# Tensor sums of a one-core mixer layer from GpSimd to VectorE, six pairs of them made early, and a new order of projections

## The chip, the core and the metric

The kernel runs on one core of one Trainium2 chip. The metric is the time of one execution on the device in microseconds; three runs of the kernel before gave 1037.36, 1037.79 and 1039.32, median 1037.79.

A core has a matrix engine (TensorE, PE in the profile; its weight loads are PEld), a vector engine (VectorE, DVE), an engine for pointwise functions (ScalarE, ACT) and a programmable one (GpSimd, POOL). Each works through its own list of instructions in the order in which the program has them, and waits on semaphores for the others. A fifth queue (SyncE, SP) issues nearly all DMAs.

## The reference

One layer over 512 tokens of width 2048, all in float32. The names in brackets are the one-letter names of the kernel's units.

```python
proj = x @ w_in                                     # (512, 2048) @ (2048, 8320)
rw, hg = proj[:, :4224], proj[:, 4224:]
rw = rw + shift_mu * (previous_token(rw) - rw)
r, k, v, z, wd, ad = split(rw)                      # [r k v z], 1024 each; [w] = wd and ad, 64 each
decay = exp(-exp(-softplus(-(w0 + tanh(wd) @ w_decay_up)) - 0.5))
a = sigmoid(a0 + ad @ a_up)
# RWKV-7, 16 heads of 64: per token S <- S * decay - (S kk)(kk a)^T + v k^T, o = S r
o_rwkv = (group_norm(o) + bonus(r, k, v)) * silu(z)
q, f, i, zh = split(hg)                             # [q f i g], 1024 each
# HGRN2, 8 heads of 128, chunks of 64 tokens: gated linear recurrence with gates from f
o_hgrn = rms_norm(hgrn2(silu(q), f, i)) * g_norm_w * silu(zh)
y = concat(o_rwkv, o_hgrn) @ w_out                  # (512, 2048) @ (2048, 2048)
out = layer_norm(2 ** 0.25 * x + y) * ln_w + ln_b
```

## The kernel before

*Products.* Every large product is made three times in a reduced float format: both factors are split into a high part (ACT copies) and a low part (DVE subtracts, line 377 through `split`), and PE adds high x high, high x low and low x high (`three`, line 524). A 128x512 tile of weights is read from DRAM into `wr`, split into `wh` and `wl`, and two parts are split ahead of the one in use. `xh` and `xl` hold the split tokens, and later the split gated channels.

*Units.* The input projection is 59 units. All but two are one tile of 128 channels over all tokens (48 large products), named by a letter and a number: `w0` (the low-rank inputs), `k`, `r`, `v`, `z` for the eight pairs of RWKV heads, `q`, `f`, `g` for the eight HGRN heads; `i0` and `i1` are four tiles each. `_order()` says in which order they are made. Their results start the other work: `rwkv_prep` (from `k`, `r`), `rwkv_group` (two pairs at a time: inversion of a triangular matrix, then the scan over eight chunks), `rwkv_finish` (needs `z`), `hgrn_heads` (from `q`, `f`), `hgrn_out` (needs `i`, `g`). Each head or pair ends as a gated tile in a buffer `g`, of which there are four; the first twelve to be used are written to DRAM (`put_gated`, tile `spill`) and read back when the output projection comes (`reload`).

*The order of the instructions* is fixed when the program is built. A class `Plan` keeps a clock for each engine, with constants for the cost of an operation, and the work is written as generators in queues. Between any two large products the planner goes through the queues and issues the instructions whose operands are ready by its clocks. The weight splits come first among the queues, the weight sums (below) last. `fetched` sets when a load is expected: 0.44 us for the issue, size over 360 GB/s, and 1.8 us more. A small product that would interrupt the large ones alone is held for up to `HOLD`, so that others can join it. For the last six units (`HURRY`) nothing is held.

*The output projection* is made in four column blocks of 512. Block 0 and block 3 are plain products. Blocks 1 and 2 are made with seven products instead of eight over blocks of tokens and of weight tiles (`PASSES`), and these need sums and differences of tiles on both sides:

- Weight sums (`weight_sums`): 16 loads of four tiles, four subtractions of 128x256 each on GpSimd (line 409 through `pool_tt`), and a store to DRAM (`sums_w`). Two generators share the work, each with one of the two `inv` buffers; the inversions use the same two buffers later.
- Token sums (`union`): for each of eight pairs of channel tiles, two tiles are read again from `spill` (the last two pairs are still in SBUF), and four sums of 128x256 are made on GpSimd. `alone` then splits them into high and low parts.
- The scaled residual 2^0.25 x is added to a partial result by `join`, eight times: ACT scales the tile `x_r` in place, GpSimd adds it.

`row_out` does the residual of the other tiles in one DVE instruction. The layer norm runs behind each row block; the last row's tail is `finish_last`.

Of the kernel before, what the change touches and what calls it, by code (L numbers as in the profile page):

```python
# [7 lines left out]
F32 = mybir.dt.float32  # L8
F32R = mybir.dt.float32r
U8 = mybir.dt.uint8  # L10
AF = mybir.ActivationFunctionType
ALU = mybir.AluOpType
# [3 lines left out]
P = 128  # L16
T = 512
# [3 lines left out]
NPAIR = 8  # L21
# [6 lines left out]
ALPHA = 2.0 ** 0.25  # L28
# [8 lines left out]

def _order():  # L40

    o = [("w", 0)]
    for g in range(NPAIR // 2):
        for p in (2 * g, 2 * g + 1):
            o += [("k", p), ("r", p)]
            if g:
                o.append(("z", p - 2))
            o.append(("v", p))
        o += [("q", 2 * g), ("f", 2 * g), ("q", 2 * g + 1), ("f", 2 * g + 1)]
        if g % 2 == 0:  # L50
            o.append(("i", g // 2))
        o += [("g", 2 * g), ("g", 2 * g + 1)]
    return o + [("z", NPAIR - 2), ("z", NPAIR - 1)]


PASSES = (("B11", "A11"), ("B21", "A12"), (3, "S2"), (0, "S1"), ("B22", "S4"), (1, "S3"), (2, "A22"))
# [8 lines left out]
class Plan:  # L65
# [4 lines left out]

    AFTER = {"pe": 0.2, "act": 0.145, "dve": 0.13, "pool": 0.06, "dma": 0.0, None: 0.1}
    TO_PE = 0.12
    HOLD = {"whole": 0.6, "narrow": 0.6}
    TURN = 0.215
    REST = 1.5
    LEAD = -0.35
# [186 lines left out]
def mixer_kernel(ctx, tc, head, x_r, w_all, par, up, ln_wb, consts, hmask, out):  # L263
# [19 lines left out]
    plan = Plan({**BUFS, **PBUFS})  # L283
# [5 lines left out]
    def take(tag, shape=(P, T), dt=F32):  # L289

        if not plan.free(tag):
            raise RuntimeError(f"no room: {tag}")
        slot = min(plan.slots[tag])
        plan.slots[tag].remove(slot)
        if tag in PBUFS:
            t = ppool.tile(list(shape), dt, tag=tag, name=nm(tag), bufs=PBUFS[tag])
            plan.banks.add(t.tensor.name)
        else:
            t = st(tag, list(shape), dt)
        name = t.tensor.name  # L300
        plan.busy[name] = (slot[1], None)
        tags[name] = tag
        return t

    def drop(*tiles):
        for t in tiles:
            name = t.tensor.name
            plan.slots[tags.pop(name)].append((plan.used.get(name, plan.count), plan.busy[name][0]))

    def room(**need):  # L310

        return lambda: all(plan.free(tag, n) for tag, n in need.items())
# [17 lines left out]
    def send(o, i, cost=0.44):  # L330

        nc.sync.dma_start(o, i)
        plan.clock["sp"] = max(plan.clock["sp"], plan.clock["pe"]) + cost
# [36 lines left out]
    def act(o, i, f, scale=1.0, bias=0.0):  # L370
        return Op([act_way(o, i, f, scale, bias)], [i], [o], SETS.get(f))
# [4 lines left out]
    def tt(o, a, b, f=ALU.mult, base=None):  # L376
        return dve_op([a, b], o, lambda: dve.tensor_tensor(o, a, b, f),  # L377
                      base=base or 0.16 if o.shape[0] < P and size(o) == C and o.tensor.name in tags else 0.07)
# [10 lines left out]
    def stt(o, a, s, b, f1, f2):  # L389
        return dve_op([a, b], o, lambda: dve.scalar_tensor_tensor(o, a, s, b, f1, f2), per=0.00113,  # L390
                      base=0.085 if o.shape[0] == P and size(o) > P else 0.12 if o.shape[0] == P
                      else 0.21 if size(o) == C else 0.165)
# [18 lines left out]
    def pool_tt(o, a, b, f):  # L411
        return Op([pool_tt_way(o, a, b, f)], [a, b], [o])
# [116 lines left out]
    def by_now(t):  # L529

        n = t.tensor.name
        return n in plan.ready and plan.seen(n, "pe") <= plan.clock["pe"] + plan.LEAD
# [141 lines left out]
    SPILL = (0, 1, 2, 3, 4, 5, 8, 9, 10, 11, 12, 13)  # L674
    spill = dpool.tile([len(SPILL), P, T], F32, tag="spill", name="spill")

    def put_gated(k, g):

        gated[k] = g
        if k in SPILL:  # L680
            def run():
                yield lambda: by_now(g)
                send(spill[SPILL.index(k)], g)
                drop(g)

            plan.add(stores, run())
# [601 lines left out]
    def weight_sums(first):  # L1288
        yield room(inv=1)
        w = take("inv", [P, 4, QT // 2])  # L1290
        for i in range(first, NSUM, 2):
            m, h = divmod(i, 2)
            yield lambda: plan.clock["sp"] <= plan.clock["pe"] + 0.2
            send(w, w_all[nsent + i].rearrange("p (a c) -> p a c", a=4))
            plan.fetched(w, 4 * HALF)
            for o, a, b in ((0, 1, 0), (1, 3, 1), (3, 3, 0), (2, 2, 3)):
                yield pool_tt(w[:, o], w[:, a], w[:, b], ALU.subtract)
            yield lambda: by_now(w)
            yield lambda: plan.clock["sp"] <= plan.clock["pe"] + 0.2
            send(sums_w[:, :, m, h * QT // 2 : (h + 1) * QT // 2].rearrange("a p c -> p a c"), w)  # L1300
            there = plan.busy[w.tensor.name] = (plan.clock["sp"] + 4.5, "dma")
            yield lambda: there[0] <= plan.clock["pe"]
        drop(w)
# [137 lines left out]
    unions, alones = [plan.queue(), plan.queue()], [plan.queue(), plan.queue()]  # L1441
    union_raw, unioned, homes = {}, {}, {}
    lnw = []
    lo_t, hi_t = slice(0, T // 2), slice(T // 2, T)

    def union(m, r1, r2):
        if m < 4:
            if m == 0:
                yield room(big=1)
                homes["raw"] = take("big", [P, 8, T])  # L1450
            d1, d2 = (homes["raw"][:, 2 * m + i] for i in range(2))
        elif m < 6:
            yield room(zz=1)
            z = homes["raw", m] = take("zz", [P, 2, T])
            d1, d2 = z[:, 0], z[:, 1]
        else:
            yield room(t=2)
            d1, d2 = homes["raw", m] = take("t"), take("t")
        if m < 6:
            yield room(t=6)  # L1460
            r1, r2 = take("t"), take("t")
            for i, r in enumerate((r1, r2)):
                yield lambda: plan.clock["sp"] <= plan.clock["pe"] + 0.2
                send(r, spill[SPILL.index(korder[2 * m + i])])
                plan.fetched(r, 4 * T)
        yield pool_tt(d2[:, hi_t], r1[:, hi_t], r2[:, hi_t], ALU.add)
        yield pool_tt(d1[:, hi_t], r1[:, lo_t], r1[:, hi_t], ALU.subtract)
        yield pool_tt(d1[:, lo_t], d2[:, hi_t], r1[:, lo_t], ALU.subtract)
        yield pool_tt(d2[:, lo_t], r2[:, lo_t], d1[:, lo_t], ALU.subtract)
        drop(r1, r2)  # L1470
        union_raw[m] = {"S1": d2[:, hi_t], "S3": d1[:, hi_t], "S2": d1[:, lo_t], "S4": d2[:, lo_t]}

    def union_home(n, m):
# [111 lines left out]
    def keyed(op, reads, writes):  # L1585

        op.reads, op.writes = reads, writes
        return op
# [188 lines left out]
    def join(o, a=None):  # L1777

        y, k = ys[o[0]][o[1]], y_keys(o[0], o[1] * T, o[1] * T + T)
        a = a or o  # L1780
        ya, ka = ys[a[0]][a[1]], y_keys(a[0], a[1] * T, a[1] * T + T)
        yield lambda: o in xrs
        xr = xrs[o]
        yield act(xr, xr, AF.Copy, scale=ALPHA)
        yield keyed(pool_tt(y, ya, xr, ALU.add), ka + [xr.tensor.name], k)
        drop(xr)
        done.add(("joined", o))
        if o in ((0, 1), (1, 1)):
            plan.add(sums, rest(*o))
# [274 lines left out]
```

## Time and profile before

| | |
|---|---|
| median of 3 runs | 1037.79 us |
| the profiled execution: its time, its span | 1039.38 us, 1037.4 us |
| instructions in the profile | 18856 |
| PE, DVE, ACT, POOL busy | 1012.2, 859.5, 499.8, 151.3 us |
| DMA | 156.99 MB, 48.9% of the engines' time in the main queue |

The profile is of one execution, with the start and the duration of each instruction. Rows of groups read: source line, engine, operation, tiles written and read (buffer numbers left out), shape, count; then busy time in us and the mean of one in ns; then how long the engine stood idle just before them and what ended it. Large products overlap by about 0.17 us, since the profile models their ends, so their starts are what tells of PE's pace.

### The profile page before, as it was taken

The numbers are of one execution on the slowest core, as the hardware profiler recorded it, in microseconds if no ns is written. First come the engines' busy times: TensorE is split into PE (matmuls) and PEld (weight loads), VectorE is DVE, ScalarE is ACT, GpSimd is POOL, SyncE is SP. The second block draws the span as 40 slices with busy tenths as digits, with TensorE's granted clock in tenths as the row PEclk, the third lists the DMA queues.
The fourth block names the chain that finished last, engine by engine and source line by source line (L and its number), as shares of the span: only waits on it lengthen the run. The fifth ranks groups of instructions, "written<-read, shape, count | busy, mean of one in ns | idle before, by whom it ended". The sixth has DMA issues, their size and how long they took to land.

```text
span 1037.4 us, 18856 instructions
## 1 busy us (share of the span) xinstructions
PE 1012.2 (98%) x7076; PEld 830.2 (80%) x7076; DVE 859.5 (83%) x1815; ACT 499.8 (48%) x945; POOL 151.3 (15%) x182
## 2 busy tenths in 40 slices
PE   9999899999999999999999999999999999999996
PEld 7877788888888878888888888888888788777785
DVE  6687779877989988888999867867998998778857
ACT  6546342546363455555544353636245554355432
POOL 2454610000200010020001000100001003732001
PEclk9999999999999999999999999999999999999999
DMA  9668862232375432255463334363442345876734
GB/s 345 225 206 250 275 203 87 83 111 69 104 213 152 120 90 68 82 143 160 130 172 104 102 93 120 100 183 102 136 115 86 112 138 158 280 227 207 225 126 152
DMA packets 75434, 156.99 MB, mean 151 GB/s; under 512 B 10960, under 2 KB 34768, under 8 KB 75344
## 3 DMA queue, kind: packets, MB, share of 16 engines
q1 hardware_dynamic: 74912, 154.89, 48.9%
q8 instruction: 55, 0.90, 0.4%
q10 hardware_dynamic: 432, 0.92, 0.2%
q14 instruction: 35, 0.29, 0.1%
HBM read 128.91 MB, written 26.87 MB: 150 GB/s over the span
## 4 chain that ended last, share of the span: by engine, by line
PE 80%; DVE 10%; DMA 4%; issue 3%; ACT 1%; POOL 1%; SPq 0%; DVEq 0%; ACTq 0%; POOLq 0%
PE main L524 64%; PE mix L353 9%; PE main L1359 3%; DVE wl L377 2%; DVE q L377 2%; PE mix L524 2%; PE main L353 2%; DMA t<-spill 1%; DMA wr<-sums_w 1%; DVE t L377 1%; DMA g<-x_r 1%; DMA q<-far 1%; DMA q<-head 1%; DVE g L390 1%; DVE ksq L377 0%
## 5 line engine op out<-in xcount | busy, mean ns | idle before, releaser
L524 PE MATMUL main<-xh,wh 128*128 128x512 f32 x864 | 340.4, 394 | 0.0
L524 PE MATMUL main<-xh,wl 128*128 128x512 f32 x864 | 339.3, 393 | 0.1
L524 PE MATMUL main<-xl,wh 128*128 128x512 f32 x864 | 339.0, 392 | 0.0
L367 ACT ACTIVATE wh<-wr 128x512 fp32r<-128x512 f32 x293 | 182.6, 626 | 177.5 <-PE main L524 131.5
L377 DVE TENSOR_TENSOR wl<-wr,wh 128x512 fp32r<-128x512 f32 x293 | 205.4, 703 | 41.6 <-ACT wh L367 39.7
L524 PEld LDWEIGHTS main<-xh,wl 128*128 128x128 f32 x864 | 162.3, 188 | 34.2 <-DVE wl L377 0.6
L524 PEld LDWEIGHTS main<-xl,wh 128*128 128x128 f32 x864 | 162.4, 188 | 33.3 <-issue 0.6
L524 PEld LDWEIGHTS main<-xh,wh 128*128 128x128 f32 x864 | 162.3, 188 | 33.1
L524 PE MATMUL main<-wl,xh 128*128 128x512 f32 x200 | 78.9, 395 | 2.7 <-DVE wl L377 2.7
L524 PE MATMUL main<-wh,xh 128*128 128x512 f32 x200 | 78.9, 395 | 0.0
L524 PE MATMUL main<-wh,xl 128*128 128x512 f32 x200 | 78.5, 392 | 0.3 <-DVE xl L377 0.3
L409 POOL TENSOR_TENSOR inv<-inv 128x256 f32<-128x256 f32 x64 | 59.8, 937 | 73.3 <-DMA inv<-w_all 69.8
L416 POOL TENSOR_TENSOR sm<-sm,mhalf 128x8 f32<-128x8 f32 x8 | 18.5, 2318 | 200.8 <-DVE sm L386 150.7
L524 PEld LDWEIGHTS main<-wl,xh 128*128 128x128 f32 x200 | 37.7, 188 | 11.4 <-DVE wl L377 3.8
L524 PEld LDWEIGHTS main<-wh,xl 128*128 128x128 f32 x200 | 37.7, 189 | 8.3 <-DVE xl L377 0.7
L524 PEld LDWEIGHTS main<-wh,xh 128*128 128x128 f32 x200 | 37.7, 188 | 7.9
L377 DVE TENSOR_TENSOR inv<-inv,inv 64x30 f32<-64x30 f32 (+14 forms) x120 | 38.5, 321 | 2.9
L377 DVE TENSOR_TENSOR inv<-inv 64x30 f32<-64x30 f32 (+14 forms) x120 | 38.5, 321 | 2.4
L390 DVE SCALAR_TENSOR_TENSOR bd<-mix,pc,bd 64x64 f32<-64x64 f32 x112 | 31.7, 283 | 10.5 <-PE mix L353 8.3
L368 ACT ACTIVATE t<-main,om 128x512 f32<-128x512 f32 x33 | 22.1, 684 | 34.6 <-PE main L524 27.2
L377 DVE TENSOR_TENSOR t<-t,tot 128x256 f32<-128x256 f32 x96 | 37.9, 417 | 0.2
L367 ACT ACTIVATE t<-mix 64x128 f32<-64x128 f32 (+3 forms) x61 | 15.8, 262 | 43.6 <-DVE zz L377 23.7
(297 smaller groups left out, 1656.0 us busy)
## 6 DMA issues: line engine op xcount, KB each, us to landing
wr<-w_all SPq DMA_DIRECT2D x146, 512.0 KB, 3.8
inv<-w_all SPq DMA_DIRECT2D x16, 512.0 KB, 4.7
sums_w<-inv SPq DMA_DIRECT2D x16, 512.0 KB, 4.4
q<-head SPq DMA_DIRECT2D x14, 448.0 KB, 5.7
t<-spill SPq DMA_DIRECT2D x23, 256.0 KB, 4.3
far<-ksq SPq DMA_DIRECT2D x22, 256.0 KB, 3.3
wr<-sums_w SPq DMA_DIRECT2D x10, 512.0 KB, 5.4
far<-q SPq DMA_DIRECT2D x8, 512.0 KB, 4.3
```

Source lines behind the costliest of these rows:

```text
L353: return Op([("pe", cost, lambda: pe.matmul(o, l, r, start=start, stop=stop, **kw))], [l, r], [o], mode=("narrow", l.shape[0], 32 if m <= ...
L367: return "act", cost, lambda: sc_e.activation(o, i, f, scale=scale)
L368: return "act", cost, lambda: sc_e.activation(o, i, f, scale=scale, bias=bias)
L377: return dve_op([a, b], o, lambda: dve.tensor_tensor(o, a, b, f), base=base or 0.16 if o.shape[0] < P and size(o) == C and o.tensor.name i ...
L390: return dve_op([a, b], o, lambda: dve.scalar_tensor_tensor(o, a, s, b, f1, f2), per=0.00113, base=0.085 if o.shape[0] == P and size(o) > ...
L409: return "pool", 0.1 + size(o) * 0.0029, lambda: pool.tensor_tensor(o, a, b, f)
L416: lambda: pool.tensor_tensor(o, i, mhalf[:, : size(o)], ALU.pow))], [i], [o])
L524: pe.matmul(ps, l, r, start=first and i == 0, stop=last and i == 2)
L1359: pe.matmul(pss[a], *ops, start=k == 0 and low == of == 0, stop=k == KT - 1 and low == 1)
```

## The change

The order of the units is a list written out, `ORDER`, in place of the loop. Before it was `w0 k0 r0 v0 k1 r1 v1 q0 f0 q1 f1 i0 g0 g1 k2 r2 z0 v2 k3 r3 z1 v3 q2 f2 q3 f3 g2 g3 k4 r4 z2 v4 k5 r5 z3 v5 q4 f4 q5 f5 i1 g4 g5 k6 r6 z4 v6 k7 r7 z5 v7 q6 f6 q7 f7 g6 g7 z6 z7`. The holds go from 0.6 to 0.3 us (products that use the whole array) and 0.4 us (narrow ones). The four subtractions of a weight sum, and the four sums of a token pair, are issued on DVE. For the six pairs whose tiles go to DRAM, the sums are made when the second tile of the pair is gated, if three scratch tiles are free by then: the first tile is read back, the sums are written in place over both, and both go to DRAM (`sums_a`). `union` then reads these in place of the tiles. `join` is one DVE instruction.

```diff
+ORDER = (
+    "w0 k0 r0 q1 k1 r1 q0 v1 f1 v0 f0 g0 i0 g1 z0 k2 f2 r2 k3 r3 "
+    "v3 z1 v2 f3 q2 q3 z2 q5 g2 g3 r4 k4 k5 v4 v5 z3 f4 r5 q4 f5 "
+    "i1 g5 g4 k6 r6 v6 v7 z4 k7 r7 f6 q7 q6 f7 g6 z6 z5 g7 z7")
+
 def _order():
...
+    return [(u[0], int(u[1:])) for u in ORDER.split()]
...
-    HOLD = {"whole": 0.6, "narrow": 0.6}
+    HOLD = {"whole": 0.3, "narrow": 0.4}
...
+    spilled, early = {}, set()
+    sums_a = dpool.tile([len(SPILL) // 2, 2, P, T], F32, tag="sums_a", name="sums_a")
+    lo_t, hi_t = slice(0, T // 2), slice(T // 2, T)
+
+    def token_sums(r1, r2, d1, d2):
+
+        yield tt(d2[:, hi_t], r1[:, hi_t], r2[:, hi_t], ALU.add)
+        yield tt(d1[:, hi_t], r1[:, lo_t], r1[:, hi_t], ALU.subtract)
+        yield tt(d1[:, lo_t], d2[:, hi_t], r1[:, lo_t], ALU.subtract)
+        yield tt(d2[:, lo_t], r2[:, lo_t], d1[:, lo_t], ALU.subtract)
...
                 send(spill[SPILL.index(k)], g)
+                now = spilled[k] = plan.clock["sp"]
+                n = korder.index(k)
+                m, other = n // 2, korder[n ^ 1]
+                if other in spilled:
+                    yield lambda: plan.free("t", 3) or plan.clock["pe"] > now + 3.0
+                    if plan.free("t", 3):
+                        r = take("t")
+                        send(r, spill[SPILL.index(other)])
+                        plan.fetched(r, 4 * T)
+                        yield lambda: plan.clock["pe"] > now + 4.5
+                        r1, r2 = (r, g) if n % 2 else (g, r)
+                        yield from token_sums(r1, r2, r1, r2)
+                        for i, r_ in enumerate((r1, r2)):
+                            yield lambda: by_now(r_) and plan.clock["sp"] <= plan.clock["pe"] + 0.2
+                            send(sums_a[m, i], r_)
+                        early.add(m)
+                        drop(r)
                 drop(g)
...
             for o, a, b in ((0, 1, 0), (1, 3, 1), (3, 3, 0), (2, 2, 3)):
-                yield pool_tt(w[:, o], w[:, a], w[:, b], ALU.subtract)
+                yield tt(w[:, o], w[:, a], w[:, b], ALU.subtract)
...
-        if m < 6:
-            yield room(t=6)
-            r1, r2 = take("t"), take("t")
-            for i, r in enumerate((r1, r2)):
+        if m in early:
+            for i, d in enumerate((d1, d2)):
                 yield lambda: plan.clock["sp"] <= plan.clock["pe"] + 0.2
-                send(r, spill[SPILL.index(korder[2 * m + i])])
-                plan.fetched(r, 4 * T)
-        yield pool_tt(d2[:, hi_t], r1[:, hi_t], r2[:, hi_t], ALU.add)
-        yield pool_tt(d1[:, hi_t], r1[:, lo_t], r1[:, hi_t], ALU.subtract)
-        yield pool_tt(d1[:, lo_t], d2[:, hi_t], r1[:, lo_t], ALU.subtract)
-        yield pool_tt(d2[:, lo_t], r2[:, lo_t], d1[:, lo_t], ALU.subtract)
-        drop(r1, r2)
+                send(d, sums_a[m, i])
+                plan.fetched(d, 4 * T)
+        else:
+            if m < 6:
+                yield room(t=6)
+                r1, r2 = take("t"), take("t")
+                for i, r in enumerate((r1, r2)):
+                    yield lambda: plan.clock["sp"] <= plan.clock["pe"] + 0.2
+                    send(r, spill[SPILL.index(korder[2 * m + i])])
+                    plan.fetched(r, 4 * T)
+            yield from token_sums(r1, r2, d1, d2)
+            drop(r1, r2)
...
-        yield act(xr, xr, AF.Copy, scale=ALPHA)
-        yield keyed(pool_tt(y, ya, xr, ALU.add), ka + [xr.tensor.name], k)
+        yield keyed(stt(y, xr, ALPHA, ya, ALU.mult, ALU.add), ka + [xr.tensor.name], k)
         drop(xr)
```

More of the change, by code (lines that the diff above doesn't have):

```diff
@@ L36 @@
     0, 33, 41, 49, 57, 65, 73, 81, 89, 97, 105)
+ORDER = (
[3 rows of a table added]
 def _order():
[L42 to L53, printed above, removed]
+    return [(u[0], int(u[1:])) for u in ORDER.split()]
 PASSES = (("B11", "A11"), ("B21", "A12"), (3, "S2"), (0, "S1"), ("B22", "S4"), (1, "S3"), (2, "A22"))
@@ L1443, in mixer_kernel, with union @@
     lnw = []
-    lo_t, hi_t = slice(0, T // 2), slice(T // 2, T)
-    def union(m, r1, r2):
+    def union(m, r1=None, r2=None):
         if m < 4:
```

## The prediction

> **What bounds the kernel now.** I read the page's busy times first, then the busy time by stage, then the list of who waited for whom, and last the order of time around the largest gaps. PE is TensorE, DVE VectorE, ACT ScalarE, POOL GpSimd, SP the queue that issues the DMAs. The first fence is the page; the second cuts the span into stages, with busy microseconds and instruction counts of PE, PEld, DVE, ACT and POOL, then the granted clock, the DMA share and GB/s; the third is the same view for POOL's tensor-tensor line alone.
>
> ```profile
> PE 1012.2 (98%) x7076; PEld 830.2 (80%) x7076; DVE 859.5 (83%) x1815; ACT 499.8 (48%) x945; POOL 151.3 (15%) x182
> ```
> ```profile
> 20.00:140.00 120.00, 112.82 (x537) 91.82 (x537) 86.92 (x120) 58.91 (x97) 60.89 (x68) 1.00 0.79 254
> 140.00:800.00 660.00, 659.69 (x5253) 546.53 (x5252) 569.86 (x1283) 318.83 (x599) 34.10 (x58) 1.00 0.41 117
> ...
> 860.00:980.00 120.00, 112.63 (x484) 88.75 (x483) 95.34 (x155) 60.52 (x121) 47.22 (x42) 0.97 0.70 224
> ```
> ```profile
> 20.00:140.00 120.00, 59.77 (x64) 1.00 0.79 254
> 140.00:800.00 660.00, 0.00 (x0) 1.00 0.41 117
> ...
> 860.00:980.00 120.00, 44.70 (x40) 0.97 0.70 224
> ```
>
> PE is the bound, and its number of matrix products does not change. So only PE's idle time and slow stretches can be won. From 140 to 800 it idles 0.3 us, although DVE is busy 86% there. It idles 120 - 112.8 = 7.2 us in 20 to 140 and 120 - 112.6 = 7.4 us in 860 to 980, and these are the two stretches in which POOL adds and subtracts tensors: 59.8 and 44.7 us of it, and none between. What PE waits for there, by the list of waits (total, times, longest), 20 to 140 first and 860 to 1020 behind it:
>
> ```profile
> PE mix L353 <- DVE ksq L377: 4.2, 3, 2.2
> PE main L353 <- DVE q L377: 2.9, 2, 1.6
> ```
> ```profile
> PE main L524 <- DVE wl L377: 5.8, 4, 2.1
> ```
>
> It always waits for a DVE result. The groups of DVE instructions, by shape, say why these are late: first 20 to 140, then 200 to 800, then 860 to 980 (busy us, mean ns | idle before).
>
> ```profile
> L377 DVE TENSOR_TENSOR wl<-wr,wh 128x512 fp32r<-128x512 f32 x33 | 26.5, 808 | 12.8 <-ACT wh L367 12.6
> ```
> ```profile
> L377 DVE TENSOR_TENSOR wl<-wr,wh 128x512 fp32r<-128x512 f32 x187 | 127.4, 681 | 16.3 <-ACT wh L367 14.7
> L377 DVE TENSOR_TENSOR t<-t,tot 128x256 f32<-128x256 f32 x64 | 24.9, 418 | 0.1
> ```
> ```profile
> L377 DVE TENSOR_TENSOR wl<-wr,wh 128x512 fp32r<-128x512 f32 x36 | 26.5, 744 | 10.5 <-ACT wh L367 10.5
> ...
> L377 DVE TENSOR_TENSOR ia<-big,ia 128x256 fp32r<-128x256 f32 x8 | 5.2, 650 | 0.0
> ```
>
> The same subtraction takes 681 ns where POOL is still, 808 and 744 ns where it works; a 256-wide one 418 against 650 ns. In order of time (start, duration), one stall of each stretch:
>
> ```profile
> 66.76 8.57 POOL L409 TENSOR_TENSOR inv<-inv 128x256 f32<-128x256 f32 x8 [5.96 <-DMA inv<-w_all]
> ```
> ```profile
> 65.59 0.69 DVE L377 TENSOR_TENSOR q<-t,pf 128x512 f32<-128x512 f32 x1
> ...
> 73.54 1.21 DVE L377 TENSOR_TENSOR q<-t,pf 128x512 f32<-128x512 f32 x1
> ```
> ```profile
> 74.80 1.16 PE L353 MATMUL main<-q,q 64*128 64x128 f32 x16 [1.26 <-DVE q L377]
> ```
> ```profile
> 945.06 1.74 POOL L409 TENSOR_TENSOR inv<-q,g 128x512 f32<-128x512 f32 x1
> ```
> ```profile
> 945.57 1.52 DVE L377 TENSOR_TENSOR ia<-big,ia 128x256 fp32r<-128x256 f32 x1
> ...
> 949.70 0.41 DVE L377 TENSOR_TENSOR ia<-big,ia 128x256 fp32r<-128x256 f32 x1
> 950.04 0.68 DVE L377 TENSOR_TENSOR wl<-wr,wh 128x512 fp32r<-128x512 f32 x1
> ```
>
> One form takes 0.69 us before POOL's burst and 1.21 us inside it, and PE waits 1.26 us for that very result. At 945 a subtraction of 0.41 us takes 1.52 us beside POOL's residual sum. The instruction order is fixed by a planner that prices a DVE instruction alike whether POOL runs or not, so PE finds itself queued behind a result that comes later than planned.
>
> Two of the late gaps also cost clock. Of 4.50 and 4.70 us just behind the gaps at 892 and 947, the granted clock was 0.62 and 0.64:
>
> ```profile
> 894.50:899.00 4.50, 4.38 (x12) 0.62 1.04 384
> ...
> 949.30:954.00 4.70, 4.50 (x13) 0.64 0.37 101
> ```
>
> That is 4.50 x 0.38 + 4.70 x 0.36 = 3.4 us.
>
> **The change part by part.** *Weight sums to DVE.* 64 instructions leave POOL (59.8 us) and join DVE. The rows at 949.70 and 950.04 start 0.34 us apart, the price of a 256-wide one in a full queue: 64 x 0.34 = 21.8 us more DVE. What goes is the stretch: by the wl group (808 - 681) / 808 = 16% of 86.9, at most 13.7 us, for not all forms stretch. DVE then has about 95 of 120 us, 79%, under the 86% at which 140 to 800 ran without a stall. Of PE's 7.2 us I take 5 as won. The ends are 7.2 won, and 16 lost, from the wait that is added: on POOL the sums stood still for their loads and held up nobody, on DVE everything behind them stands still too. These rows carry it, groups of instructions and DMA issues (KB each, median us to landing):
>
> ```profile
> L409 POOL TENSOR_TENSOR inv<-inv 128x256 f32<-128x256 f32 x64 | 59.8, 937 | 73.3 <-DMA inv<-w_all 69.8
> ```
> ```profile
> inv<-w_all SPq DMA_DIRECT2D x16, 512.0 KB, 4.7
> ```
>
> The planner expects such a load after 0.44 + 1.46 + 1.8 = 3.7 us (its own constants), so the median load is 1 us late: 16 us of DVE standing still if none of the 16 were covered. I take the cover as good for most, since DVE still has 25 us free there and the weight splits are made two parts ahead. Queued behind are those splits and the score operands; PE waits for them.
>
> *Token sums of six pairs, early.* 24 instructions x 0.34 = 8.2 us of DVE move to before the output stage, where DVE has 660 - 570 = 90 us free and PE 0.3 us of idle: 0, and 8.2 us if that cover were gone. SP gets 6 more loads (the pair's first half comes back) and 12 more stores of 256 KB, 4.7 MB beside 157 moved at a DMA share of 0.41: 0. A gated tile now holds its g buffer until the sums are stored, three transfers instead of one; behind it stand the finish of the next head and the other spills, which PE meets only in the output stage: 0. In that stage 12 loads stay 12, but land as sums: 24 POOL instructions and their 6 pairs of scratch tiles go, and the ACT and DVE splits behind them come earlier.
>
> *Last two pairs and the residuals.* 8 sums x 0.34 = 2.7 us, and 8 joins each one DVE instruction in place of one of ACT and one of POOL:
>
> ```profile
> L367 ACT ACTIVATE g<-g 128x512 f32<-128x512 f32 x8 | 4.9, 617 | 0.0
> ```
> ```profile
> L390 DVE SCALAR_TENSOR_TENSOR q<-g,main 128x512 f32<-128x512 f32 x3 | 2.1, 688 | 5.2 <-DMA g<-x_r 5.2
> ```
>
> 8 x 0.69 = 5.5 us of DVE. The new wait, for x_r, is what held DVE 5.2 us in the second row; but the eight scalings never stood idle for theirs (0.0 in the first), so 0 here. Against 8.2 us added stands the stretch removed: 36 x 0.063 (wl) + 8 x 0.24 (ia) = 4.2 us in these two groups, which hold 31.7 of the 95.3 busy us; some 12 in all if the rest stretch alike. DVE does not get busier, and its longest instructions fall from 1.5 to 0.7 us. The gap at 892 hangs on POOL too: its last instruction on the pair in g frees the buffer into which x_r is loaded, and DVE waits for that before the weight split behind it.
>
> ```profile
> 888.30 0.75 POOL L409 TENSOR_TENSOR t<-t,g 128x256 f32<-128x256 f32 x1
> ```
> ```profile
> 889.08 2.42 SPq L332 DMA_DIRECT2D g<-x_r  x2
> ```
> ```profile
> 892.17 0.69 DVE L390 SCALAR_TENSOR_TENSOR q<-g,main 128x512 f32<-128x512 f32 x1 [4.42 <-DMA g<-x_r]
> ```
>
> Of 7.4 + 3.4 = 10.8 us I take 9 as won: the four POOL-bound gaps and the clock go, some waiting for late loads stays. Ends: 10.8 and 4. The Trainium skill (TensorE: Matmul & The Clock Gate, What's actually happening) puts the fall to half clock at about 3.4 us of idleness; the gaps here were near 2 us and a slow stretch followed all the same. By the page these stretches would not hang on the gaps and would stay; the trace speaks against it, and I go by the trace.
>
> *Shorter holds.* The planner lets a lone small product wait 0.3 or 0.4 us instead of 0.6 for company, so bursts may split. One burst costs, by starts (64 small products among the large):
>
> ```profile
> 654.56 0.39 PE L524 MATMUL main<-xh,wh 128*128 128x512 f32 x1
> 654.79 0.39 PE L524 MATMUL main<-xl,wh 128*128 128x512 f32 x1
> 655.11 2.09 PE L353 MATMUL mix<-zz,big 128*64 128x64 f32 x64
> 657.12 0.50 PE L524 MATMUL main<-xh,wl 128*128 128x512 f32 x1
> 657.46 0.39 PE L524 MATMUL main<-xh,wh 128*128 128x512 f32 x1
> ```
>
> The large ones start 0.23 apart, here 0.32 before and 0.34 behind the burst: 0.2 us for one. Twenty more bursts cost 4 us. Steps of the scans gain up to 0.3 us each, off PE's path; in the last six units, where they would count, nothing is held before or after. I take +0.5 us, between -1 and +4.
>
> *The order.* The same 59 units, so PE's work is the same. Nothing in the trace shows another order; I bound it by the last group's chain (below) and take 0.
>
> Sum: -5 - 9 + 0.5 = -13.5. The profiled execution took 1039.4 us (span 1037.4 and 2.0 around it), 1.6 above the median of the runs, 1037.8; so 1025.9 for it and 1024.3 for a median: 1024.
>
> **The rivals.** *The last group is late* (1031). Before, ten units follow the last r (r7), now nine, one unit of 48 x 0.23 = 11 us less for inversion, scan and finish of heads 12 to 15. That chain had no slack:
>
> ```profile
> 731.75 0.75 DVE L390 SCALAR_TENSOR_TENSOR t<-main,pr,t 128x511 f32<-128x511 f32 x1 [0.91 <-ACT t L368]
> ```
> ```profile
> 879.82 0.68 DVE L377 TENSOR_TENSOR xl<-g,xh 128x512 fp32r<-128x512 f32 x1
> ```
> ```profile
> 880.55 0.50 PE L524 MATMUL main<-wh,xl 128*128 128x512 f32 x1 [0.27 <-DVE xl L377]
> ```
>
> It runs 148 us from r7's eviction to the split for which PE waits. If none of it can be shortened, PE idles 11 us more near 870; if a third of the 11 is waiting for a turn, 7, and 1024 + 7 = 1031. Against it: two pairs' z and two heads' f and q are made in that time, and how much of the 148 us is queueing the trace does not tell.
>
> *Slower: DVE stands behind the loads* (1041). Place: 20 to 200 us. If all 16 us of lateness reach PE and the 5 are not won, 1024 + 5 + 16 = 1045; with three quarters of it, 1041. It decides at (13.5 - 5) / 16 = 0.53 us for each load: where more of it reaches PE, the kernel is slower. For: PE's small products follow their operands closely. Against: the 25 us free.
>
> *More is won* (1016): all 18 us of both stretches and 4 less lost at bursts by another grouping (20 bursts fewer x 0.2), 1038 - 18 - 4. *The clock stays* (1027): the two slow stretches have another cause than the gaps before them, and their 3.4 us are not won, 1024 + 3.4; against it, both lie right behind a gap. That is what the clock-gate page of the Trainium skill would make of gaps this short. *No change* (1037): the stalls are the planner's landing times, and others take their place; against it, no stall of 140 to 800, with the same kind of loads.
>
> **How the numbers follow.** Forecast 0.44, last group late 0.16, more won 0.16, slower 0.12, clock stays 0.07, no change 0.05. Faster: 0.44 + 0.16 + 0.16 + 0.07 = 0.83; same 0.05 (within 0.2%, 2 us, about what a measurement of this kernel can tell from none); slower 0.12. The range 1014 to 1034 leaves out the slower case and no change, 0.17; the likeliest case alone spans 1019 to 1029 by the ends of its terms.
>
> **What would show it.** POOL's tensor-tensor line nearly gone; wl near 690 ns in every stage; no PE wait over 1 us for DVE in 860 to 980 and the clock 1.00 there; PE idle in 20 to 140 under 3 us. Wrong would be: DVE idle released by loads of inv in 20 to 200 with PE waits behind them; PE idle near 870 behind xl; more bursts with PE's idle unchanged.

## The result and the profile after

The changed kernel took 1026.74 us (median of 4 runs, 1025.14 to 1028.26), the kernel before beside it 1037.64 us: a ratio of 0.9891 with an interval of 0.9872 to 0.9910. The forecast was 1024, the range 1014 to 1034. The profiled execution of the kernel after took 1025.14 us (span 1022.4) and was the fastest of its four, that of before (1039.38, span 1037.4) the slowest; so the spans differ by 15.0 us where the medians differ by 10.9.

The page of the kernel after, then its busy time by stage in the columns of the prediction (PE, PEld, DVE, ACT, POOL, granted clock, DMA share, GB/s):

```profile
PE 1006.3 (98%) x7076; PEld 828.9 (81%) x7076; DVE 860.8 (84%) x1889; ACT 510.0 (50%) x968; POOL 42.4 (4%) x78
```
```profile
20.00:140.00 120.00, 119.60 (x632) 98.45 (x631) 93.31 (x180) 61.46 (x102) 1.04 (x3) 1.00 0.69 227
140.00:800.00 660.00, 657.82 (x5241) 544.49 (x5241) 572.44 (x1292) 330.53 (x629) 28.45 (x56) 1.00 0.45 129
860.00:980.00 120.00, 116.41 (x506) 93.50 (x505) 97.42 (x181) 61.16 (x120) 1.14 (x1) 1.00 0.76 243
```

POOL is nearly idle and DVE as busy as before, with 74 instructions more. The stretches are cut by time, so in the late one the faster kernel is some microseconds further on in the same work. PE idles 0.4 us in 20 to 140 (before 7.2), 3.6 in 860 to 980 (before 7.4, and the clock is 1.00 where it was 0.97), and 2.2 in 140 to 800 (before 0.3). The groups of DVE, 20 to 140 first and 860 to 980 behind it (busy us, mean ns | idle before):

```profile
L372 DVE TENSOR_TENSOR wl<-wr,wh 128x512 fp32r<-128x512 f32 x36 | 24.6, 686 | 5.4 <-ACT wh L362 5.2
L372 DVE TENSOR_TENSOR inv<-inv 128x256 f32<-128x256 f32 x56 | 23.2, 422 | 10.9 <-DMA inv<-w_all 10.0
```
```profile
L372 DVE TENSOR_TENSOR wl<-wr,wh 128x512 fp32r<-128x512 f32 x36 | 24.6, 687 | 10.3 <-ACT wh L362 10.1
...
L372 DVE TENSOR_TENSOR ia<-big,ia 128x256 fp32r<-128x256 f32 x8 | 3.4, 419 | 0.0
```

The weight split `wl` is back at 686 and 687 ns (808 and 744 before), `ia` at 419 (650). DVE now stands 10.0 us for the loads of `inv`, the thing that the slower rival was about. The list of waits of the kernel after (total, times, longest; PE's two for DVE in the late stretch, then DVE's):

```profile
PE mix L519 <- DVE wl L372: 1.5, 3, 0.9
...
PE main L519 <- DVE t L372: 1.0, 1, 1.0
```
```profile
DVE inv L372 <- DMA inv<-w_all: 11.6, 7, 3.9
```
```profile
inv<-w_all SPq DMA_DIRECT2D x16, 512.0 KB, 5.5
```

Those loads landed after a median of 5.5 us, later than before (4.7), and DVE stood still up to 3.9 us; PE hardly noticed. So the signs that the prediction named are there: POOL's sums gone, `wl` near 690 ns, no wait of PE for DVE over 1 us in the late stretch and the clock 1.00 there, PE's idle time under 3 us in the early one.

### The profile page after: what moved, and what is told of

The parts are those of the page before. It is cut to its first block, busy times and chain, and to the rows that moved or that the text cites. A ratio compares the mean times of both kernels' runs of the same rounds, so it can differ in the third digit from the quotient of the medians.

```text
span 1022.4 us, 18865 instructions
## 1 busy us (share of the span) xinstructions
PE 1006.3 (98%) x7076; PEld 828.9 (81%) x7076; DVE 860.8 (84%) x1889; ACT 510.0 (50%) x968; POOL 42.4 (4%) x78
## 4 chain that ended last, share of the span: by engine, by line
PE 81%; DVE 9%; DMA 6%; issue 2%; ACT 1%; SPq 0%; POOL 0%; DVEq 0%; ACTq 0%
PE main L519 66%; PE mix L348 9%; PE main L1382 3%; DVE wl L372 2%; PE main L348 2%; DVE q L372 1%; PE mix L519 1%; DMA wr<-w_all 1%; DMA inv<-w_all 1%; DMA wr<-sums_w 1%; DVE t L372 1%; DVE inv L372 1%; DMA g<-x_r 1%; DMA q<-head 1%; ACT wh L362 1%
## 5 line engine op out<-in xcount | busy, mean ns | idle before, releaser
L372 DVE TENSOR_TENSOR wl<-wr,wh 128x512 fp32r<-128x512 f32 x293 | 199.8, 683 | 33.3 <-ACT wh L362 31.2
L372 DVE TENSOR_TENSOR inv<-inv 128x256 f32<-128x256 f32 (+10 forms) x184 | 65.0, 355 | 14.9 <-DMA inv<-w_all 11.6
L519 PE MATMUL main<-wh,xh 128*128 128x512 f32 x194 | 76.3, 393 | 0.2
L519 PE MATMUL main<-wl,xh 128*128 128x512 f32 x194 | 76.0, 392 | 0.2 <-DVE wl L372 0.2
L519 PE MATMUL main<-wh,xl 128*128 128x512 f32 x194 | 75.9, 391 | 0.0
L362 ACT ACTIVATE t<-mix 64x128 f32<-64x128 f32 (+3 forms) x74 | 19.1, 261 | 40.5 <-DVE zz L372 28.1
L363 ACT ACTIVATE t<-main 128x512 f32<-128x512 f32 x32 | 18.8, 597 | 27.3 <-PE main L519 27.2
L385 DVE SCALAR_TENSOR_TENSOR t<-main,pr,t 128x511 f32<-128x511 f32 x33 | 24.2, 744 | 9.0 <-ACT t L363 8.9
```

The lines of the kernel that those rows point to most:

```text
L362: return "act", cost, lambda: sc_e.activation(o, i, f, scale=scale)
L363: return "act", cost, lambda: sc_e.activation(o, i, f, scale=scale, bias=bias)
L519: pe.matmul(ps, l, r, start=first and i == 0, stop=last and i == 2)
```

## The experiments

While it writes the list of instructions, the planner's clocks run; where TensorE's clock stands at the end is called the *planned end* below. It is a number of the program, not a time of the chip, and it knows nothing of one engine slowing another. Span minus planned end is what the chip adds, idle or not. The spans are those of the profiled executions, one each: that of the kernel with the weight sums on GpSimd lies 5 us above its kernel's median, that with fills in the kernel after 4. The ratios compare runs that were made together.

| kernel | median us | ratio to before, interval | span | planned end | difference |
|---|---|---|---|---|---|
| before | 1037.64 | | 1037.4 | 1005.2 | 32.2 |
| after | 1026.74 | 0.9891, 0.9872 to 0.9910 | 1022.4 | 1005.6 | 16.8 |
| before, GpSimd only fills | 1025.87 | 0.9867, 0.9840 to 0.9895 | 1022.5 | 1005.2 | 17.3 |
| engines alone | 1040.66 | 1.0017, 1.0001 to 1.0032 | 1038.5 | 1018.2 | 20.3 |
| weight sums alone | 1043.61 | 1.0044, 1.0031 to 1.0058 | 1041.7 | 1013.7 | 28.0 |
| token sums and residuals alone | 1034.08 | 0.9958, 0.9941 to 0.9976 | 1031.2 | 1006.8 | 24.4 |
| order and holds alone | 1083.54 | 1.0415, 1.0387 to 1.0443 | 1083.0 | 1071.5 | 11.5 |
| after, no early sums | 1037.75 | 0.9983, 0.9969 to 0.9997 | 1035.2 | 1011.6 | 23.6 |
| after, old order | 1037.40 | 0.9978, 0.9966 to 0.9991 | 1035.1 | 1019.0 | 16.1 |
| after, old holds | 1073.58 | 1.0323, 1.0299 to 1.0347 | 1071.2 | 1071.3 | -0.1 |
| after, weight sums on GpSimd | 1056.69 | 1.0170, 1.0138 to 1.0203 | 1060.0 | 1041.0 | 19.0 |
| after, POOL reads at 704 to 840 | 1038.26 | 0.9985, 0.9973 to 0.9996 | 1037.0 | 1005.6 | 31.4 |
| after, POOL fills there | 1023.86 | 0.9867, 0.9848 to 0.9886 | 1026.5 | 1005.6 | 20.9 |
| after, loads expected later | 1020.49 | 0.9813, 0.9786 to 0.9840 | 1021.3 | 1007.0 | 14.3 |

The kernels before and after are planned to the same time. All 15 us between their spans stand in the last column.

### The parts by themselves

*Engines alone.* The kernel before with all sums and residuals on DVE; order, holds and the time of the sums untouched.

```diff
-                yield pool_tt(w[:, o], w[:, a], w[:, b], ALU.subtract)
+                yield tt(w[:, o], w[:, a], w[:, b], ALU.subtract)
...
-        yield pool_tt(d2[:, hi_t], r1[:, hi_t], r2[:, hi_t], ALU.add)
+        yield tt(d2[:, hi_t], r1[:, hi_t], r2[:, hi_t], ALU.add)
...
-        yield act(xr, xr, AF.Copy, scale=ALPHA)
-        yield keyed(pool_tt(y, ya, xr, ALU.add), ka + [xr.tensor.name], k)
+        yield keyed(stt(y, xr, ALPHA, ya, ALU.mult, ALU.add), ka + [xr.tensor.name], k)
```

> The kernel before with old order and old holds; all 64 weight-sum instructions, all 32 token-sum instructions (none of them early) and the 8 residual joins go to VectorE. Contention theory (PE stalls because GpSimd's tensor-tensor instructions stretch the VectorE instructions beside them): most of the gain is here, PE idle in 20 to 140 us from 7.2 to under 3 us, wl at 690 ns or less in every stage, time 1025 to 1031. Order theory (the new order and the shorter holds make the gain): 1036 to 1040. Early-sums theory (the token sums that leave the output stage make it): PE idle in the output stage stays near 7 us or grows, since 24 sums more stand on VectorE there; 1031 to 1036.

1040.66 us: no gain, and 10 us above the 1025 to 1031 that the theory of contention gave, though its sign came: PE idles 1.7 us in 20 to 140. Two new holes take the place of the old stalls. Its list of waits, the busy time of the 15 us around the first hole, and in order of time the second:

```profile
PE main L524 <- ACT t L367: 5.2, 1, 5.2
PE main L353 <- DVE t L390: 5.0, 1, 5.0
```
```profile
470.00:485.00 15.00, 10.01 (x44) 8.00 (x43) 14.90 (x30) 4.06 (x7) 6.58 (x5) 0.89 0.34 115
```
```profile
921.67 0.90 SPq L332 DMA_DIRECT2D t<-spill  x2
...
926.77 0.43 DVE L377 TENSOR_TENSOR zz<-t,t 128x256 f32<-128x256 f32 x1 [1.68 <-DMA t<-spill]
928.84 0.42 ACT L367 ACTIVATE t<-zz 128x256 fp32r<-128x256 f32 x1 [5.40 <-DVE zz L377]
...
929.31 0.80 PE L524 MATMUL main<-wh,t 128*128 128x512 f32 x1 [5.15 <-ACT t L367]
```

At 479 DVE is busy 14.9 of 15 us and PE waits for an eviction (a result copied out of PE's output memory) in its queue. No weight sum is near; the list has come out otherwise. At 924 the chain is read whole: reload, sums, split, product, 929.31 - 921.67 = 7.6 us, and PE has nothing else. The planned end went up by 13.0 us and what the chip adds fell by 11.9 (32.2 to 20.3): what was won against the chip is lost again in a longer list. That DVE's longer queue makes the list longer is read from these rows; no run tests it alone.

*Weight sums alone*, and *token sums and residuals alone*: the first, or the second and third, of the hunks above in the kernel before.

> The kernel before with the 64 weight-sum instructions on VectorE and nothing else. Contention theory: PE idle in 20 to 140 us falls from 7.2 to under 3, the output stage keeps its 7 us and its slow clock; 1031 to 1034. Load theory (VectorE stands behind late loads of the sums' tiles): VectorE idle released by those loads of 8 to 16 us and PE idle of 5 us or more in 20 to 200 us; 1037 to 1045.

> The kernel before with the 32 token-sum instructions and the 8 joins on VectorE, none of the sums early; weight sums stay on GpSimd. Contention theory: the first stretch keeps 7 us of PE idle, the output stage loses most of its 7.4 us and its slow clock; 1028 to 1033. Early-sums theory: moving the sums to VectorE inside the output stage loads it by 8 us more there and wins less than 2 us; 1036 to 1039.

1043.61 and 1034.08 us. The first lies in the range of the rival about loads (1037 to 1045), but not for its reason: DVE stood 11.9 us for the loads of `inv` in 20 to 200, and PE idled 1.2 us there. The second lies between its two ranges. By stage, weight sums alone first, then the other:

```profile
20.00:140.00 120.00, 118.80 (x565) 97.16 (x564) 92.17 (x176) 61.08 (x101) 1.03 (x3) 1.00 0.71 232
860.00:980.00 120.00, 109.72 (x471) 86.03 (x469) 89.20 (x151) 59.06 (x119) 44.05 (x42) 0.97 0.68 213
```
```profile
20.00:140.00 120.00, 113.36 (x541) 92.52 (x540) 85.60 (x119) 57.96 (x96) 59.25 (x68) 1.00 0.78 254
860.00:980.00 120.00, 113.71 (x505) 91.50 (x505) 103.25 (x203) 60.03 (x118) 2.52 (x2) 1.00 0.74 235
```

The weight sums cure the early stretch (PE idles 1.2 us) and leave the late one (10.3 us). The token sums and residuals leave the early one (6.6 us), and in the late one they win the clock (1.00) but hardly any idle time: 6.3 us where it was 7.4, although `wl` takes 686 ns there. PE waits there 2.4 us for `wl`, 1.8 for `wh` and 1.5 for split token sums, and DVE is busy 103 us of 120. The hole at 479 comes with the weight sums, and it is the same one:

```profile
PE main L353 <- DVE t L390: 5.0, 1, 5.0
```

*Order and holds alone*, in the kernel before:

```diff
-    HOLD = {"whole": 0.6, "narrow": 0.6}
+    HOLD = {"whole": 0.3, "narrow": 0.4}
...
+    return [(u[0], int(u[1:])) for u in ORDER.split()]
```

> The kernel before with the new order and the shorter holds alone; every sum stays on GpSimd. Contention theory: both stretches keep their stalls, PE idle of 5 to 9 us in each and wl over 740 ns there; 1033 to 1041. Order theory: 1025 to 1030 with the stalls of 20 to 140 us gone although wl is still stretched.

1083.54 us, 4% slower and far outside both ranges. The late stretch, and the longest wait:

```profile
860.00:980.00 120.00, 92.44 (x564) 71.26 (x563) 85.40 (x163) 48.58 (x107) 39.80 (x43) 0.77 0.44 140
```
```profile
PE main L519 <- ACT xh L362: 16.1, 2, 15.2
```

PE idles 28 us there and waits 15.2 us for one split of a gated tile: in this list the last group comes late, the very rival of the prediction, though not in the kernel that was predicted.

### The parts undone

*No early sums* (`if other in spilled:` made `if False:`), *old order* (`_order()` of before), *old holds* (`HOLD` 0.6 and 0.6), and *weight sums on GpSimd* (`pool_tt` in `weight_sums`; `reload` also waits until its tile has been written to `spill`, so two things differ), each in the kernel after.

> The changed kernel without the early token sums: the tiles are read back in the output stage and all 32 sums stand on VectorE there, as in the run with engines alone. Theory now (VectorE moved with the old order runs into two new holes, one of them the chain load of spill, sums, splits in the output stage): PE waits of 4 to 7 us in 900 to 935 us behind a split of a token sum return; 1030 to 1036. Rival (the order alone closed both holes): output stage unchanged, 1025 to 1028.

> The changed kernel with the order of before; engines, early sums and shorter holds stay. Theory now (the new order spreads the VectorE work that piles up when the order of before gets 22 us more of it): a PE wait of about 5 us near 480 us behind VectorE returns, the output stage stays clean; 1030 to 1036. Rival (holds and early sums are what helps, the order is neutral): 1024 to 1028 with no wait over 2 us between 140 and 800 us.

> The changed kernel with the holds of before (0.6 and 0.6 us). Theory (order and holds fit one set of costs; with others the planner's list falls apart): the planner's own clock ends at 1071 us instead of 1006, with PE idle near 880 to 930 behind the last group, so 1080 to 1095 us measured. Rival (holds are worth a few bursts, as I predicted, -4 to +1): 1022 to 1028.

> The changed kernel with only the weight sums back on GpSimd. Theory: two things add up, the planner's clock, which ends 35 us later (1041 against 1006, idle near 810 to 900), and the stretched DVE of 20 to 140 (PE idle there 5 to 8 us, wl near 800 ns): 1062 to 1075 us. Rival (the weight sums are worth the early stall alone, everything else stays): 1031 to 1035.

All four lose against the kernel after: 1037.75, 1037.40, 1073.58 and 1056.69 us. None lies in a range that was expected: the first two are 1 to 2 us above theirs, 1073.6 lies under 1080 to 1095, 1056.7 between its two ranges. Of the signs, the wait behind a split of token sums came, the wait of about 5 us near 480 with the old order did not. The waits that the changed lists bring, in that order (of the second kernel two):

```profile
PE main L519 <- ACT t L362: 7.4, 2, 5.8
```
```profile
PE mix L353 <- DVE t L390: 3.5, 3, 1.8
...
PE mix L358 <- DVE t L377: 2.3, 1, 2.3
```
```profile
PE main L519 <- ACT xh L362: 18.1, 2, 16.1
```
```profile
PE mix L519 <- ACT xh L362: 13.1, 1, 13.1
```

Without the early sums the chain of the engines-alone kernel is back: PE waits 5.8 us for a split of token sums. With the old order there is no such wait; the planned end is 13.4 us later than that of the kernel after and the span 12.7 us longer, so the loss lies in the list itself. With the old holds, or the weight sums elsewhere, the last group is late again by 16.1 and 13.1 us. In the kernel with the weight sums back on GpSimd the early stretch shows the stalls of before besides, by stage and by group:

```profile
20.00:140.00 120.00, 115.52 (x551) 94.42 (x550) 84.66 (x118) 59.49 (x99) 62.42 (x68) 1.00 0.75 242
```
```profile
L372 DVE TENSOR_TENSOR wl<-wr,wh 128x512 fp32r<-128x512 f32 x34 | 28.5, 842 | 10.4 <-ACT wh L362 10.1
```

So order, holds and early sums can't be priced one by one: with any one of them put back, the planner's list falls out otherwise, and by the ratios 9 to 45 us are lost against the kernel after. With the old holds the planned end is 65.7 us later (1071.3) and the span 48.8 us longer: the late list was visible when the program was built.

### What the stalls were

*GpSimd reads, GpSimd fills.* In the kernel after, from about 704 us for 40 weight parts, GpSimd does useless work on a tile that nobody uses: either two subtractions of 128x256, or five fills of it. An 8-column instruction ties each to the weight split just made. The order of the other engines is untouched, and the planned end is the same.

```diff
+            pool.tensor_tensor(j[:, 0:8], j[:, 0:8], lo[:, 0:8].bitcast(F32), ALU.mult)
+            for _ in range(2):                                 # the other kernel: range(5)
+                pool.tensor_tensor(j, j, j, ALU.subtract)      # the other kernel: pool.memset(j, 0.0)
```

> The changed kernel with 80 useless GpSimd subtractions of 128x256 (and 40 of 128x8 that tie them in time) added beside the last twelve projections, from about 720 us on, two for each weight part; their results go nowhere. The instructions of all other engines and their order stay. Contention theory: wl in that stretch goes from 685 to 760 ns or more, PE idle grows by 4 to 12 us, time 1030 to 1038. Rival (GpSimd beside VectorE costs nothing, the stalls of before were landing times): wl stays, 1025 to 1028.

> As the run with useless GpSimd subtractions, but five memsets of 128x256 for each part in place of the two subtractions: GpSimd is about as busy and only writes. If reading is what collides: wl stays near 685 ns and the time within 0.3% of the changed kernel, 1025 to 1029. If any work of GpSimd stretches VectorE, or if it is the queueing of GpSimd's own instructions behind the added ones that costs: as the subtractions, 1030 or more.

1038.26 and 1023.86 us, ratios 0.9985 and 0.9867: the reads undo nearly all that the change won, the fills cost nothing. (The first lies 0.3 us above its range, the second 1.1 under.) The pages of the two, reads first:

```profile
PE 1014.3 (98%) x7076; PEld 832.1 (80%) x7076; DVE 875.1 (84%) x1889; ACT 508.4 (49%) x968; POOL 118.0 (11%) x199
```
```profile
PE 1007.9 (98%) x7076; PEld 830.6 (81%) x7076; DVE 860.5 (84%) x1889; ACT 509.1 (50%) x968; POOL 120.1 (12%) x319
```

From 720 to 860, by stage and by group: reads, fills, and the kernel after.

```profile
720.00:860.00 140.00, 132.68 (x1203) 107.46 (x1203) 130.33 (x286) 60.62 (x131) 67.06 (x112) 0.98 0.37 112
```
```profile
L541 POOL TENSOR_TENSOR up<-up 128x256 f32<-128x256 f32 x68 | 52.8, 777 | 5.3
...
L372 DVE TENSOR_TENSOR wl<-wr,wh 128x512 fp32r<-128x512 f32 x37 | 26.1, 704 | 1.0 <-ACT wh L362 0.6
...
L372 DVE TENSOR_TENSOR inv<-inv 64x238 f32<-64x238 f32 x2 | 1.6, 807 | 0.0
```
```profile
720.00:860.00 140.00, 138.46 (x1254) 114.76 (x1253) 127.63 (x306) 67.31 (x142) 74.10 (x217) 1.00 0.43 129
```
```profile
L541 POOL MEMSET up<- 128x256 f32 x170 | 54.7, 322 | 9.8
...
L372 DVE TENSOR_TENSOR wl<-wr,wh 128x512 fp32r<-128x512 f32 x42 | 28.6, 681 | 2.4 <-ACT wh L362 1.5 <-POOL up L541 0.5
...
L372 DVE TENSOR_TENSOR inv<-inv 64x238 f32<-64x238 f32 x2 | 0.8, 396 | 0.0
```
```profile
720.00:860.00 140.00, 139.15 (x1257) 115.24 (x1256) 128.14 (x308) 68.10 (x144) 8.23 (x14) 1.00 0.44 131
```

GpSimd is busy 67 and 74 us of 140. Over the whole run the same 1889 DVE instructions take 875.1 us beside the reads and 860.5 beside the fills (860.8 in the kernel after). Beside the reads two DVE instructions of 64x238, one of the groups that are stretched most, take 807 instead of 396 ns, and PE idles 139.15 - 132.68 = 6.5 us more in that stretch, at clock 0.98; beside the fills neither happens. The sign that was named missed: `wl` went to 704 ns and not to 760. Each burst of reads waits for the weight split just made, and other forms carry most of the stretch. So it is not GpSimd's being busy that slows DVE. What differs is that the subtractions read their tile and the fills don't; no run has GpSimd calculate without reading. The Trainium skill (SBUF — State Buffer, Who interferes with whom) has this rule: a DVE instruction with two inputs in SBUF contends with a GpSimd instruction that reads SBUF, not with one that only writes. The trace agrees, with these 807 against 396 ns.

*Before, without its reads.* The kernel before with its own order, holds, engines and loads; each sum on GpSimd becomes an 8-column instruction that reads the same tiles, and two fills of the output. Left out: the sums themselves.

```diff
+        def writes():
+            pool.tensor_tensor(o[:, 0:8], a[:, 0:8], b[:, 0:8], f)
+            for _ in range(2):
+                pool.memset(o, 0.0)
+
+        return Op([(way[0], way[1], writes)], [a, b], [o])
```

> The kernel before, its instruction order untouched; each of GpSimd's sums (weights, tokens, residuals) is replaced by an 8-column instruction that reads the same tiles and two fills with zeros of the same output, so GpSimd is about as busy at the same places and nearly never reads SBUF (the sums are not computed). Theory (DVE is stretched while GpSimd reads SBUF, and that is all of the stalls of before): wl near 685 ns in every stage, PE idle in 20 to 140 falls from 7.2 to 2 us or less, in 860 to 980 from 7.4 to 4 or less with the clock at 1.00, and the time is 1023 to 1028 us although neither order nor holds nor the engine of the sums changed. Rival (the stalls hang on late loads and on the order, and the change won by its new order): the stalls stay and the time is 1034 to 1038.

1025.87 us, a ratio of 0.9867: the whole gain of the change, with nothing of the change in it. The page, two stages, and the groups of 20 to 140:

```profile
PE 1007.1 (98%) x7076; PEld 828.6 (81%) x7076; DVE 831.4 (81%) x1815; ACT 499.7 (49%) x945; POOL 147.9 (14%) x392
```

```profile
20.00:140.00 120.00, 117.94 (x564) 97.12 (x563) 76.11 (x127) 63.25 (x104) 62.02 (x196) 1.00 0.82 260
...
860.00:980.00 120.00, 118.58 (x515) 94.63 (x514) 92.19 (x168) 65.45 (x130) 41.93 (x122) 1.00 0.76 248
```
```profile
L419 POOL MEMSET inv<- 128x256 f32 x128 | 40.6, 317 | 7.5
L377 DVE TENSOR_TENSOR wl<-wr,wh 128x512 fp32r<-128x512 f32 x35 | 23.6, 684 | 16.0 <-ACT wh L367 13.7 <-PE main L533 1.8
```

POOL is as busy as before in both stretches (62.0 and 41.9 us; 60.9 and 47.2), the same 1815 DVE instructions take 831.4 us instead of 859.5, and PE idles 2.1 and 1.4 us instead of 7.2 and 7.4, at clock 1.00 (2 or less and 4 or less were expected). The rival, that the stalls came from late loads and the old order, is out: the order is still there, and the loads of `inv` land after a median of 4.6 us (4.7 before). The early stretch is the cleaner of the two. In the late one GpSimd is 5.3 us less busy, and products of sums have zeros as factors; no run parts these from the missing reads. Late, it makes a difference how the stretch of DVE is lifted: 1.4 us of idle time where the work stays on GpSimd, 6.3 where it goes to DVE's queue in the output stage.

### A version that beats both

The idea: what the kernel after still adds to its planned end may partly be PE waiting behind operands that came from loads. In this version `fetched` expects every load 1 us later.

```diff
-        self.ready[tile.tensor.name] = (self.clock["dma"] + 1.8, "dma")
+        self.ready[tile.tensor.name] = (self.clock["dma"] + 2.8, "dma")
```

> The changed kernel; the planner expects every load 1 us later (2.8 instead of 1.8 us behind the transfer). Its own clock ends at 1007 instead of 1006. Theory (what the changed kernel still loses, 17 us more than planned, is partly loads that land later than planned): PE waits behind loads shrink, PE idle in 860 to 980 from 3.6 to 2 us or less, in 140 to 800 from 2.2 to 1, and the time is 1021 to 1025 us. Rival (what is left is spread over the pace of products and bursts): within 2 us of the changed kernel, 1025 to 1029.

1020.49 us (1018.93 to 1023.12), just under the 1021 to 1025 expected. Its interval (0.9786 to 0.9840) lies below that of the change, though the two were not timed together; the profiled spans are 1.1 us apart, this one's from the slowest of its runs and the other's from the fastest. By stage:

```profile
20.00:140.00 120.00, 120.00 (x634) 98.82 (x633) 93.76 (x183) 60.92 (x102) 1.03 (x3) 1.00 0.71 229
140.00:800.00 660.00, 656.64 (x5163) 542.17 (x5164) 574.90 (x1304) 324.49 (x614) 28.78 (x56) 1.00 0.44 128
...
860.00:980.00 120.00, 118.26 (x513) 94.54 (x512) 100.06 (x186) 60.87 (x120) 1.61 (x2) 1.00 0.76 243
```

PE idles 0.0 us early and 1.7 late, as expected, but 3.4 in 140 to 800 where 1 was expected. That it is faster is shown; that later expected loads are the reason, and not just another list, is not.

## Why the prediction was right, and which steps were not

*The cause* (DVE stretched beside GpSimd, PE behind late results) is shown, twice: put into the kernel after, GpSimd's reads take it from 0.9891 back to 0.9985 of before; taken out of the kernel before, they bring it to 0.9867.

*Weight sums to DVE*: 5 of 7.2 us were taken as won, 6.8 came (7.2 - 0.4). DVE went to 93.3 us of the stretch (about 95 reckoned). The end of -16 us was far off: DVE stood 10.0 us for those loads and PE idled 0.4 in all. That the splits are made ahead would explain it; no run took that lead away.

*The late stretch*: 9 of 10.8 taken, 7.2 came: 3.8 of idle (7.4 - 3.6) and 3.4 of clock. That is between the ends of 10.8 and 4. The move to DVE alone would not have brought it: with the sums and residuals on DVE but not early, the clock came back and 6.3 of the 7.4 us of idle time stayed.

*Early token sums*: 0 was taken, with 90 us of free DVE as the cover. The cover held but for 1.9 us (PE idle in 140 to 800 from 0.3 to 2.2). But as a part it is worth 9.5 us, (0.9983 - 0.9891) x 1037.6: it keeps a chain like the 7.6 us one of reload, sums and split out of the output stage. I had counted that gain under the late stretch, as if moving the sums to DVE alone would bring it. The kernels with the engines alone and with the token sums alone show that it doesn't.

*Holds* (+0.5, between -1 and +4) and *the order* (0): these two steps failed, and by the most. Old holds in the changed kernel cost 44.8 us, (1.0323 - 0.9891) x 1037.6, the old order 9.0; both new ones in the kernel before cost 43.1 (0.0415 x 1037.6). I priced a burst and a unit, and what they change is the whole list, whose planned end moves by 13 to 66 us. The terms don't add: by the ratios the engines alone bring +0.2%, order and holds alone +4.2%, and with the early sums all together -1.1%.

The total came out since the list that went with the change is as long as that of before (planned ends 1005.6 and 1005.2), which I assumed and had no row for: that part was luck. Given two equal lists, what was left is the contention, and that I had read from the trace. Of the span's 15.0 us the stages give 6.8 + 3.8 + 3.4 - 1.9, and 800 to 860 some 0.7: 12.8. The other 2.2 were not found in one place; over the whole span PE idles 16.1 us instead of 25.2 and is busy 5.9 us less, of which the clock explains 3.4.

*The rivals.* The last group was not late: no wait for `xl` stands among PE's. It was late in three kernels with parts of the change, by 13 to 16 us. The slower one did not happen, as above. The clock did not stay: the gaps went and the slow stretches with them.

## What to carry to other kernels

Where one form of DVE instruction has two durations, look for what GpSimd reads at that time; a page of groups by shape, cut at GpSimd's bursts, shows it in three rows, and a run in which GpSimd only fills prices it. Moving the work to the engine that was slowed is only half of it: DVE's queue gets the work too, and it has to be made at a time when DVE is free. With a planner whose list is chosen for one set of costs, don't price an order or a hold by its own instructions; price it by whether the new list, as a whole, waits longer.

## What the runs showed of the hardware

GpSimd's fill of 128x256 takes 317 and 322 ns in the two kernels above and leaves DVE's total where it was (860.5 against 860.8 us). Its subtraction of that size takes 777 ns beside DVE's work, and DVE's two instructions of 64x238 take 411 ns more beside it. Forms with one input in PE's output memory (`main`, `mix`) kept their time, inside a burst too (`t<-main,pr,t` at 51.60 us took 0.75, GpSimd's burst ran from 51.38 to 55.36): in 20 to 140 of the kernel before, `t<-main,pr,t` took a mean of 743 ns and `big<-mix,cst` 673, and 745 and 680 where GpSimd only fills, while `q<-t,pf` took 948 and 682. Nor is every other instruction in a burst stretched: in GpSimd's burst from 105.77 to 110.11 us `q<-t,pf` took 1.21 us and a weight split 0.68.

The granted clock does not follow the length of a gap near 2 us. By stage, around the two largest late gaps of the kernel with token sums and residuals alone on DVE, and around one gap of the kernel in which GpSimd fills:

```profile
890.00:900.00 10.00, 7.87 (x34) 5.86 (x33) 8.19 (x16) 4.36 (x9) 0.00 (x0) 1.00 0.97 297
903.00:910.00 7.00, 5.01 (x21) 3.54 (x21) 4.81 (x10) 4.62 (x9) 0.00 (x0) 1.00 0.75 258
```
```profile
898.00:908.00 10.00, 7.68 (x26) 5.61 (x25) 6.97 (x15) 6.87 (x16) 0.00 (x0) 0.83 0.56 185
```

PE idles 2.1 and 2.0 us in the first two, and the clock is 1.00; it idles 2.3 us in the third, and the clock is 0.83. The longest single gaps in them are 1.66, 1.76 and 2.09 us, and that of the kernel before at 892, behind which the clock was 0.62, is 1.76 us as well. So my price for such a gap (3.4 us for two) was that of this one list and not a rule. The Trainium skill (TensorE: Matmul & The Clock Gate, What's actually happening) has a window of about 3.4 us that runs by itself, so that where a gap falls in it would matter; that would fit these rows, but no run here moved a gap to see.
